# Log-sum-exp of 16,384 rows on one core: another list of loads (twenty in place of nineteen), with other groups of rows for each engine

## The chip, the core and the metric

The kernel runs on one core of a Trainium2 chip. The core's engines run side by side, each with its own instruction stream, and meet through semaphores: ScalarE (ACT in the profile) does exponentials and logarithms, VectorE (DVE) sums, GpSimd (POOL) adds, TensorE (PE) has only three tiny products at the end, and SyncE (SP) issues the transfers from memory. The metric is the time of one execution on the device in microseconds; lower is better.

## The reference

```python
x = np.random.randn(32, 512, 1024).astype(np.float32)

max_x = np.max(x, axis=-1, keepdims=True)
out = max_x.squeeze(-1) + np.log(np.sum(np.exp(x - max_x), axis=-1))
```

There are 32 x 512 = 16,384 rows of 1024 floats, 67.1 MB, and one float comes out per row. The kernel sums exp(x) without the maximum, checks at the end that all sums lie within sane bounds, and has a second, slower way with the maximum that runs only where the check fails. With this input it isn't run.

## The kernel before, in words

The 16,384 rows are spread over the 128 partitions of the on-chip memory, 128 rows to a partition. Below, "a row" is one row in every partition: 1024 elements wide, 512 KB in all. Rows 0 to 111 of each partition come from one block of the input (`x_rows`), rows 112 to 127 from a second (`x_rest`).

The plan is a list, `LOADS`, of pairs: how many rows a transfer brings (fractions are allowed, in steps of 1/32), and in a string what is done with rows once they are there. A load may end within a row; the next one brings the rest. The loop over the list (`for i, (size, parts) in enumerate(loads)`) writes out the instruction streams of all engines:

- **SyncE** issues one transfer per load (line 143), in the list's order, into `ring`, a buffer of 48 rows (`RING`). Loads are laid one behind the other; where the next does not fit any more, it goes to the ring's start. Before it issues a load, SyncE waits until every earlier row in that space has been summed (the list `users`). All loads go through one queue and their data move in the order of issue.
- **ScalarE** waits for a load to land and puts exp over it in place (line 231), in one instruction for each part of the string that the load's text has, separated by blanks. A `+` joins several groups in one exponential, with the groups behind it. The last part of a load takes all that has landed, fractions of a row included.
- **Letters.** `R9`: VectorE sums nine whole rows with one reduction (line 242). `G7`: GpSimd adds the second half of seven rows to the first (line 237), and a later `H` makes VectorE sum the halves of all groups folded until then (line 161); only then is their ring space free. `T2`: VectorE adds the halves of a row and sums them in one `scalar_tensor_tensor` per row (line 169). `C`: VectorE checks the sums so far, two small reductions (line 178). `L`: ScalarE takes the logarithm of rows 0 to 111 (line 204), for which it waits until VectorE has summed the last of them; SyncE then stores these results early, after all loads. `a` and `b`: the two pieces of the last row; VectorE sums the first, and ScalarE sums the second as it takes its exponential (line 226).

At load number `HELD` (counted from 0) VectorE waits, before its T instruction, for the next load to land too.

Behind the loop come the logarithms of the last 16 rows (lines 269 and 271), the store, and the check of the sums: lines 280 and 284 on VectorE, three products on TensorE (lines 290 to 294) and the comparison of line 298. Each engine works its instructions in the order in which they are written: a ScalarE instruction that waits holds up all behind it. Nothing plans at run time; the list is the whole schedule.

Of the kernel before, what the change touches and what calls it, by code (L numbers as in the profile page):

```python
# [10 lines left out]
RING = 48  # L11
B = 16

HELD = 15

# [2 lines left out]


LOADS = [
# [5 lines left out]
]  # L28


# [23 lines left out]
def kernel(  # L54
# [127 lines left out]
    for i, (size, parts) in enumerate(loads):  # L182
# [8 lines left out]
        for k, part in enumerate(parts):  # L191
# [41 lines left out]
            for how, s in part:  # L233
# [12 lines left out]
                elif how == "T":  # L246
                    if i == HELD:
                        nc.vector.wait_ge(landed[i + 1], 16)
# [161 lines left out]
```

## Time and profile before

| | us |
|---|---|
| median of 3 runs | 161.41 (161.4 to 161.55) |
| the profiled execution | 161.56 |
| its span | 160.2 |
| VectorE busy | 116.1 |
| ScalarE busy | 114.5 |
| GpSimd busy | 33.3 |
| transfers into and out of the core, 67.18 MB | mean 419 GB/s over the span |

The span runs from the first recorded instruction to the last; about 1.3 us of the execution lie around it. Rows of the timeline give the start and the duration in us, engine, line, operation, output and input with their sizes, how many instructions the row holds, and in brackets the engine's idle time before it with what ended it. A row that stands for several instructions names the first one's size. GpSimd and ScalarE rows name the elements per partition: 1024 for a whole row, 512 for a half. The stage rows give, for each stretch, busy time and instruction count of PE, PEld (TensorE's loading of weights), DVE, ACT and POOL, the clock granted to TensorE, the busy share of the DMA engines and the GB/s.

### The profile page before, as it was taken

What the parts mean: (1) busy time and instruction counts of PE and PEld (TensorE: products, weight loads), DVE (VectorE), ACT (ScalarE), POOL (GpSimd) and SP (SyncE); (2) the same over time, 40 slices, a digit from 0 to 9 for tenths busy, and PEclk for the clock granted to TensorE, in tenths of its full rate; (3) what the DMA queues carried; (4) which work ended last, traced back from release to release, by engine and by line L of the source; (5) the groups of instructions that cost most, each with busy time, mean ns of one, the idle gap of its engine ahead of it and who ended that gap; (6) DMA issues with size and microseconds to landing.
All of it is one profiled execution on the core that took longest, in us unless ns stands there. A gap on an engine that the chain in (4) does not pass through costs nothing.

```text
span 160.2 us, 183 instructions
## 1 busy us (share of the span) xinstructions
PE 0.3 (0%) x6; PEld 0.2 (0%) x6; DVE 116.1 (72%) x56; ACT 114.5 (71%) x32; POOL 33.3 (21%) x14
## 2 busy tenths in 40 slices
PE   0000000000000000000000000000000000000000
PEld 0000000000000000000000000000000000000000
DVE  0000000029998499999999799929989999999996
ACT  3000069970899519992799449964998999999996
POOL 0000000000000000000000000990580489996000
DMA  8999799799699699997999999997999999999992
GB/s 288 479 511 431 336 514 450 321 514 497 272 512 512 288 463 478 478 448 312 424 467 467 467 429 429 429 429 332 498 426 409 415 440 394 438 419 425 417 408 101
DMA packets 3025, 67.18 MB, mean 419 GB/s; under 512 B 592, under 2 KB 720, under 8 KB 1488
## 3 DMA queue, kind: packets, MB, share of 16 engines
q1 hardware_dynamic: 3024, 67.18, 97.9%
q14 instruction: 1, 0.01, 0.0%
HBM read 67.11 MB, written 0.07 MB: 419 GB/s over the span
## 4 chain that ended last, share of the span: by engine, by line
DMA 54%; DVE 21%; ACT 19%; POOL 5%; issue 0%; PE 0%; SPq 0%
DMA ring<-in_x_dram 54%; ACT ring L231 19%; DVE sumexp L242 15%; POOL ring L237 5%; DVE ring L169 3%; DVE sumexp L161 2%; SPq L143 0%; DVE clamped L280 0%; PE count L290 0%; ACT res L204 0%; DVE fine L298 0%; PE count L292 0%; PE count L294 0%
## 5 line engine op out<-in xcount | busy, mean ns | idle before, releaser
L231 ACT ACTIVATE ring<-ring 128x16000 f32<-128x16000 f32 (+24 forms) x25 | 112.2, 4546 | 42.8 <-DMA ring<-in_x_dram 42.8
L242 DVE TENSOR_REDUCE sumexp<-ring 128x9 f32<-128x9216 f32 (+7 forms) x10 | 89.8, 9000 | 39.2 <-ACT ring L231 39.2
L237 POOL TENSOR_TENSOR ring<-ring 128x2048 f32<-128x2048 f32 (+5 forms) x8 | 33.0, 4135 | 112.3 <-ACT ring L231 112.3
L161 DVE TENSOR_REDUCE sumexp<-ring 128x4 f32<-128x2048 f32 (+5 forms) x8 | 16.5, 2080 | 3.5 <-POOL ring L237 3.5
L169 DVE SCALAR_TENSOR_TENSOR ring<-ring 128x512 f32<-128x512 f32 (+1 forms) x16 | 9.8, 671 | 0.0
L130 ACT ACT_TABLE_LOAD x1 | 1.3, 1283 | 1.4 <-PEq L63 1.4
L169 DVE DVE_READ_ACCUMULATOR ring<-ring 128x1 f32 x16 | 1.3, 82 | 0.0
L226 ACT ACTIVATE unused<-ring 128x480 f32<-128x480 f32 x1 | 0.6, 559 | 0.0
L290 PE MATMUL count<-far,bad 128*1 128x1 f32 x2 | 0.2, 164 | 158.7 <-DVE clamped L280 158.7
L178 DVE TENSOR_REDUCE sumexp<-sumexp 128x1 f32<-128x106 f32 x2 | 0.4, 258 | 0.0
L298 DVE TENSOR_SCALAR fine<-count 1x1 int32<-1x1 f32 x1 | 0.1, 146 | 0.3 <-PE count L294 0.3
L131 POOL MEMSET ones<- 128x1 f32 x1 | 0.1, 98 | 1.0 <-POOLq L63 1.0
L290 PEld LDWEIGHTS count<-far,bad 128*1 128x1 f32 x2 | 0.1, 80 | 158.7 <-DVE clamped L280 158.7
L204 ACT ACTIVATE res<-sumexp 128x112 f32<-128x112 f32 x1 | 0.3, 279 | 0.0
L271 ACT ACTIVATE res<-rest,sumexp 128x1 f32<-128x1 f32 x1 | 0.3, 261 | 0.0
L280 DVE SCALAR_TENSOR_TENSOR clamped<-sumexp 128x23 f32<-128x23 f32 x1 | 0.2, 183 | 0.0
L269 ACT ACTIVATE res<-sumexp 128x15 f32<-128x15 f32 x1 | 0.2, 205 | 0.0
L292 PE MATMUL count<-total,ones 128*1 128x1 f32 x2 | 0.2, 164 | 0.0
L294 PE MATMUL count<-sumexp,ones 128*1 128x1 f32 x2 | 0.2, 164 | 0.0
L284 DVE TENSOR_REDUCE total<-sumexp 128x1 f32<-128x24 f32 x1 | 0.2, 173 | 0.0
L274 ACT COPY sumexp<-rest 128x1 f32<-128x1 f32 x1 | 0.2, 152 | 0.0
L394 POOL MEMSET const-float32-0.0<- 128x1 f32 x1 | 0.1, 98 | 0.2 <-issue 0.2
(8 smaller groups left out, 0.8 us busy)
## 6 DMA issues: line engine op xcount, KB each, us to landing
ring<-in_x_dram SPq DMA_DIRECT2D x1, 8048.0 KB, 39.1
ring<-in_x_dram SPq DMA_DIRECT2D x1, 8016.0 KB, 57.6
ring<-in_x_dram SPq DMA_DIRECT2D x1, 8000.0 KB, 21.5
ring<-in_x_dram SPq DMA_DIRECT2D x1, 7472.0 KB, 25.8
ring<-in_x_dram SPq DMA_DIRECT2D x1, 7312.0 KB, 22.9
ring<-in_x_dram SPq DMA_DIRECT2D x1, 6720.0 KB, 21.5
ring<-in_x_dram SPq DMA_DIRECT2D x1, 5200.0 KB, 17.6
ring<-in_x_dram SPq DMA_DIRECT2D x1, 3584.0 KB, 19.1
```

What stands on the lines that cost most here:

```text
L130: nc.scalar.preload_act_table_set("natural_log_exp_and_others")
L161: at = dve.did(nc.vector.reduce_sum(out=sumexp[:, c0 : c0 + s], in_=half, axis=AX.X))
L169: return nc.vector.scalar_tensor_tensor(out=lo, in0=lo, scalar=1.0, in1=v[:, h : 2 * h], op0=ALU.mult, op1=ALU.add, accum_out=sumexp[:, co ...
L178: dve.did(nc.vector.tensor_reduce(out=sumexp[:, col : col + 1], in_=sumexp[:, 0:c], op=op, axis=AX.X))
L204: ln_early = act.did(nc.scalar.activation(out=res[:, 0:W], in_=sumexp[:, 0:W], func=AF.Ln))
L226: nc.scalar.activation(out=unused[:, 0 : upto - here], in_=v, func=AF.Exp, accum_out=rest).then_inc(parts_summed, 1)
L231: at = act.did(nc.scalar.activation(out=v, in_=v, func=AF.Exp))
L237: folded.append((c, p, s, pool.did(nc.gpsimd.tensor_tensor(out=rows[:, :, 0:H], in0=rows[:, :, 0:H], in1=rows[:, :, H:d], op=ALU.add,))))
L242: users.append((p, p + s * d, dve, dve.did(nc.vector.reduce_sum(out=sumexp[:, c : c + s], in_=rows, axis=AX.X))))
L269: act.did(nc.scalar.activation(out=res[:, W:LAST], in_=sumexp[:, W:LAST], func=AF.Ln))
L271: ln_last = act.did(nc.scalar.activation(out=res[:, LAST:NC], in_=rest, func=AF.Ln, bias=sumexp[:, LAST:NC]))
L290: pe.did(nc.tensor.matmul(count, lhsT=bad, rhs=far, start=True, stop=False))
```

## The change

The list is another. The ring, the letters and the code behind the list are the same.

```diff
-HELD = 15
+HELD = 16
...
 LOADS = [
-    (15.625, "R15"), (15.71875, "R16"), (15.65625, "R9 R7"), (14.59375, "R14"),
-    (14.28125, "G7 H R7"), (13.125, "G5 H R9"), (10.15625, "G4 H R3+G3 H"), (7, "G4 R2 H G1"),
-    (5.84375, "H C G2+R1 G3 H"), (4.46875, "T4"), (3.09375, "T3 L"), (2.40625, "T2"),
-    (1.75, "T2"), (1.25, "T1"), (0.75, "T1"), (0.65625, "T1"), (0.625, "T1"), (0.53125, "a"),
-    (0.46875, "b"),
+    (15.71875, "R15"), (15.3125, "R16"), (15.96875, "R16"), (14.5625, "G5 R9 H"),
+    (15.625, "R7+G2 R7 H"), (10.8125, "R11"), (7.5, "G5 G2"), (8.0625, "H G5 R3"),
+    (4.03125, "G3 G1 H C"), (4.40625, "G1 T4 H"), (4.3125, "R2+G2 L H"), (3.03125, "T3"),
+    (2.40625, "T2"), (1.6875, "T2"), (1.3125, "T1"), (0.96875, "T1"), (0.75, "T1"),
+    (0.59375, "T1"), (0.5, "a"), (0.4375, "b"),
 ]
```

There are 20 loads; the first three fill 47 rows of the ring as before, the next three now 41 (before 42), and the list goes to the ring's start twice, as before. Of the 127 rows that are not split, VectorE sums 86 with whole-row reductions (before 83), GpSimd folds 26 (before 29), its first at load 3 (before load 4), and 15 are T rows in both; four of these now come in load 9, ahead of the groups of load 10. Load 2 is one group of 16 rows, with one exponential, in place of nine and seven. The early logarithm `L` stays in load 10, which now holds two whole and two folded rows in place of three T rows. The check at the end takes one column less, since the early check `C` covers one more row.

## The prediction

> **What bounds the kernel now.** First the page's span and busy times, then the timeline of ScalarE alone, because every load is first touched by an exponential there: a row that ends its idle time on the DMA tells when a load was ready.
>
> ```profile
> span 160.2 us, 183 instructions
> ...
> PE 0.3 (0%) x6; PEld 0.2 (0%) x6; DVE 116.1 (72%) x56; ACT 114.5 (71%) x32; POOL 33.3 (21%) x14
> ```
>
> ```profile
> 21.56 13.54 ACT L231 ACTIVATE ring<-ring 128x16000 f32<-128x16000 f32 x1 [18.83 <-DMA ring<-in_x_dram]
> 40.54 13.62 ACT L231 ACTIVATE ring<-ring 128x16096 f32<-128x16096 f32 x1 [5.45 <-DMA ring<-in_x_dram]
> 59.45 13.66 ACT L231 ACTIVATE ring<-ring 128x8864 f32<-128x8864 f32 x2 [5.29 <-DMA ring<-in_x_dram]
> 77.09 12.66 ACT L231 ACTIVATE ring<-ring 128x14944 f32<-128x14944 f32 x1 [3.98 <-DMA ring<-in_x_dram]
> 94.34 12.48 ACT L231 ACTIVATE ring<-ring 128x6560 f32<-128x6560 f32 x2 [4.60 <-DMA ring<-in_x_dram]
> 110.25 11.50 ACT L231 ACTIVATE ring<-ring 128x4224 f32<-128x4224 f32 x2 [3.42 <-DMA ring<-in_x_dram]
> 122.53 15.22 ACT L231 ACTIVATE ring<-ring 128x4096 f32<-128x4096 f32 x5 [0.79 <-DMA ring<-in_x_dram]
> 138.08 5.28 ACT L231 ACTIVATE ring<-ring 128x2912 f32<-128x2912 f32 x2 [0.33 <-DMA ring<-in_x_dram]
> 143.52 6.75 ACT L231 ACTIVATE ring<-ring 128x4576 f32<-128x4576 f32 x2 [0.16 <-DMA ring<-in_x_dram]
> 150.18 0.28 ACT L204 ACTIVATE res<-sumexp 128x112 f32<-128x112 f32 x1
> 150.37 7.55 ACT L231 ACTIVATE ring<-ring 128x2464 f32<-128x2464 f32 x7
> 157.82 0.56 ACT L226 ACTIVATE unused<-ring 128x480 f32<-128x480 f32 x1
> 158.31 0.13 ACT L226 ACTIVATION_READ_ACCUMULATOR unused<-ring 128x1 f32 x1
> ```
>
> The transfers never pause. Load 1 (15.71875 rows) becomes ready 18.98 us after load 0, load 2 (15.65625) 18.91 us later, load 4 (14.28125) 17.25 us after load 3, load 6 (10.15625) 12.28 us after load 5. One straight line fits: 1.2055 us a row and 0.04 us a load (15.71875 x 1.2055 + 0.04 = 18.99; 10.15625 x 1.2055 + 0.04 = 12.28). From load 9 (143.52) to load 18 lie 11.53 rows in nine loads, by the line 14.26 us, so the last is ready at 157.78 at the earliest; ScalarE starts it at 157.82. The bound is the queue of loads, not an engine: the end is 157.8 plus a tail that nearly cannot shrink. What a change of the list can do is delay the queue (a load issued too late) or lengthen the tail (an engine behind when the last load lands).
>
> The tail is two paths. ScalarE's ends at 158.31 + 0.13 = 158.44. VectorE's, from its own timeline:
>
> ```profile
> 157.40 0.69 DVE L169 SCALAR_TENSOR_TENSOR ring<-ring 128x512 f32<-128x512 f32 x1
> 158.01 0.08 DVE L169 DVE_READ_ACCUMULATOR ring<-ring 128x1 f32 x1
> 158.01 0.44 DVE L169 SCALAR_TENSOR_TENSOR ring<-ring 128x272 f32<-128x272 f32 x1
> ```
>
> It ends at 158.45. Behind both stand 1.75 us of checks and control to 160.2. So the span is (later of the two paths) + 1.75. The profiled execution took 161.56 us for its span of 160.2; the median of the runs is 161.41, 0.15 below it. I work out a difference in span and put it on 161.41.
>
> **The change, part by part: the queue.** The same 128 rows come in 20 loads instead of 19: + 0.04 us by the line. Between no cost and what an issue not hidden would cost (bounded below), 0.04 is what nineteen loads showed. Ready times in the changed kernel are 21.56 + (rows loaded - 15.625) x 1.2055 + 0.04 x load number: load 2 at 59.46, load 3 77.05, load 4 95.93, load 5 109.00, load 6 118.09, load 7 127.85, load 8 132.75, load 9 138.10, load 10 143.34, then 147.04, 149.98, 152.05, 153.67, 154.88, 155.82, 156.58, 157.22 and 157.79 for load 19.
>
> That holds if SyncE issues each load before the queue reaches it, which hangs on ring space freed by VectorE. Its rows, and the page's issue rows for loads 4 and 5:
>
> ```profile
> 35.13 16.15 DVE L242 TENSOR_REDUCE sumexp<-ring 128x15 f32<-128x15360 f32 x1 [35.13 <-ACT ring L231]
> 54.19 34.41 DVE L242 TENSOR_REDUCE sumexp<-ring 128x16 f32<-128x16384 f32 x3 [2.91 <-ACT ring L231]
> 89.78 15.09 DVE L242 TENSOR_REDUCE sumexp<-ring 128x14 f32<-128x14336 f32 x1 [1.18 <-ACT ring L231]
> 107.91 3.89 DVE L161 TENSOR_REDUCE sumexp<-ring 128x7 f32<-128x3584 f32 x1 [3.05 <-POOL ring L237]
> 111.72 7.61 DVE L242 TENSOR_REDUCE sumexp<-ring 128x7 f32<-128x7168 f32 x1
> 119.73 2.82 DVE L161 TENSOR_REDUCE sumexp<-ring 128x5 f32<-128x2560 f32 x1 [0.41 <-POOL ring L237]
> 122.47 9.75 DVE L242 TENSOR_REDUCE sumexp<-ring 128x9 f32<-128x9216 f32 x1
> ...
> 141.43 2.87 DVE L161 TENSOR_REDUCE sumexp<-ring 128x4 f32<-128x2048 f32 x2
> 144.34 0.43 DVE L178 TENSOR_REDUCE sumexp<-sumexp 128x1 f32<-128x106 f32 x2
> 144.69 1.21 DVE L242 TENSOR_REDUCE sumexp<-ring 128x1 f32<-128x1024 f32 x1
> ```
>
> ```profile
> ring<-in_x_dram SPq DMA_DIRECT2D x1, 7312.0 KB, 22.9
> ring<-in_x_dram SPq DMA_DIRECT2D x1, 6720.0 KB, 21.5
> ```
>
> Before, load 4 (7312 KB) was under way for 22.9 us though it takes 17.25: 5.6 us of it in the queue; load 5 likewise 21.5 - 15.9 = 5.6. That is the spare now. After: load 2 is one R16 in place of R9 and R7, so ScalarE works it in one piece. By its rows (13.62 for 16096 elements, 12.66 for 14944: 0.833 ns an element and 0.2 us) that ends at 59.46 + 13.82 = 73.28, and VectorE, idle from about 70.7, reduces 16 rows in 17.22 (1.07 us a row + 0.12, from 9.75 for 9 and 7.61 for 7) to 90.5. Load 5 waits for exactly this and the queue needs it at 95.93: 5.4 us spare. Load 4 needs the first R16, about 70.7 (load 1 is 0.4 us earlier ready), against 77.05. Load 6 needs R9 and the folded five of load 3: 90.5 + 9.67 + 2.8 = 102.9 against 109.00. Loads 11 to 19 need R11, about 131.4, against 143.34 and later. So no load starves. VectorE's 2.6 us of idle time in front of R16 are covered by these spares; without them each microsecond beyond would shift the end by one. SyncE's own row before:
>
> ```profile
> 132.24 10.66 SPq L143 DMA_DIRECT2D ring<-in_x_dram  x7
> ```
>
> Seven issues in 10.66 us, 1.5 each; nine from 131.4 at that pace end at 145.1, twelve microseconds before the last is needed. The early store is queued behind them; it is issued after L204, 147.3 in place of 150.5, and in both kernels its data stand in the queue behind the last load.
>
> **VectorE up to the early logarithm.** L204 now stands in load 10 and waits for the last folded row of load 9, and behind it on ScalarE are the eight exponentials of loads 11 to 18 and the last, which everything waits for. So VectorE's chain counts. Steps from the rows above, an instruction starting 0.08 before its forerunner ends (107.91 + 3.89 = 111.80 against 111.72): R of n rows 1.07n + 0.04; H of n folded rows 0.535n + 0.065 (3.89 for 7, 2.82 for 5); the early check 0.47 (the reduction before it ends at 144.30, less the 0.08, to 144.69); a T row 0.61. The chain starts when ScalarE has done the R7+G2 piece of load 4, 8640 elements: 95.93 + 7.40 + 0.03 = 103.36. Then R7 7.53, R7 7.53, H2 1.14, R11 11.81, H5 2.74, H2 1.14, R3 3.25, H5 2.74, H3 1.67, H1 0.60, check 0.47, T4 2.44, H1 0.68 with its end: 43.74, ending at 147.10. GpSimd has to keep up:
>
> ```profile
> 100.09 7.79 POOL L237 TENSOR_TENSOR ring<-ring 128x3584 f32<-128x3584 f32 x1 [98.52 <-ACT ring L231]
> ...
> 131.57 11.57 POOL L237 TENSOR_TENSOR ring<-ring 128x1536 f32<-128x1536 f32 x4 [0.78 <-ACT ring L231]
> 143.44 3.44 POOL L237 TENSOR_TENSOR ring<-ring 128x1536 f32<-128x1536 f32 x1 [0.29 <-ACT ring L231]
> ```
>
> That is 1.09 us a row + 0.18. G5 of load 7 starts when ScalarE's 4608 elements are done, 131.96, and ends at 137.6, G3 141.0, the two G1 142.25 and 143.5; VectorE comes to H3 at 141.24, 0.2 later. R3's exponential ends at 135.02, VectorE comes at 135.25. So the chain holds, with 0.2 us at its two tightest places.
>
> **ScalarE to the end.** A step is 0.833 ns an element + 0.1 us: the row of seven has 8160 elements, 6.80 us, in 7.55. Load 10 starts at 143.34, its 4416 elements step to 147.12; L204 needs VectorE's 147.10 + 0.03 = 147.13: nothing lost. L204 steps 0.19 (150.18 to 150.37), to 147.32. Then 3104 to 150.01, 2464 to 152.16, 1728 to 153.70, 1344 to 154.92, 992 to 155.84, 768 to 156.58, 608 to 157.18 (load 18 is ready at 157.22), 512 to 157.75, and the last load at 157.79: ScalarE is 0.3 us behind at load 11 and caught up by load 18. Its path ends 0.62 - 0.03 (32 elements fewer) later, at 158.38. VectorE: T of load 16 at 156.68, T of load 17 at 157.30 to 157.92, the half row of load 18 in 0.45: 158.37. The wait moved from load 15 to 16 (for load 17 to land, 156.58) is over before ScalarE hands over that row at 156.65; it costs nothing.
>
> **Sum.** 158.38 against 158.45: - 0.07 us. 161.41 - 0.07 is 161.34; I say 161.35, no change that a measurement tells from none (within 0.2%, 0.32 us, is about what it can).
>
> **A rule of the skill.** T4 in load 9 is the change's riskiest move by row: its `scalar_tensor_tensor` runs right behind GpSimd's last G1 (143.98 against 143.5), while before the first T, behind the rows above, came 1.7 us after GpSimd's last end at 146.88. The Trainium skill, page "SBUF — State Buffer", section "Who interferes with whom", says that a VectorE instruction with two SBUF inputs and a GpSimd instruction that reads SBUF lock each other out for a whole instruction, while a reduction does not contend. The trace of before agrees as far as it goes: R9 beside GpSimd took 9.75, as its rate elsewhere; it has no T beside GpSimd. By the rule and by the rows the sum is the same as long as the two keep those 0.5 us apart; where they do not, the rule gives rival 2.
>
> **The rivals.** (1) Slower: VectorE's 43.7 us chain runs late and L204 holds ScalarE. It decides from 0.1 us of lateness on (0.03 at load 18, 0.04 at the last load), then one to one; 1% of the chain, 0.44, gives 161.7, 1 us of it 162.25; I take 161.9. For it: the two 0.2 us spares, no idle time after 103.4. Against: reductions in the trace go by one line. (2) Slower: GpSimd is late by over 0.5 us and T4 and G1 exclude each other; H1 then ends up to one G1 later (1.27): 161.8 to 162.5. Nothing in the trace makes GpSimd late, and no row of before shows the two side by side. (3) Slower: the queue pays for the added load or for late space. The nearest row for a price from above is an issue's 1.5 us: 162.9; against it stands the 0.04 and the 5.4 us spare. (4) Faster: the queue loses time in the middle, which other sizes recover:
>
> ```profile
> 94.34:110.25 15.91, 0.00 (x0) 0.00 (x0) 12.86 (x2) 12.49 (x3) 7.79 (x1) 1.00 0.97 420
> 110.25:122.53 12.28, 0.00 (x0) 0.00 (x0) 11.87 (x4) 11.49 (x2) 5.65 (x1) 1.00 0.97 419
> ```
>
> A DMA share of 0.97 over 28.2 us would be 0.85 us, giving at best 160.5. Against it: these stages keep to the line within 0.05 us.
>
> **How the numbers follow.** The forecast has 0.75, (1) 0.10, (2) 0.05, (3) 0.04, (4) 0.06. The likeliest case's own range is 161.2 to 161.6; the range 161.15 to 161.95 takes in most of rival 1 and leaves out about 2 in 10. Faster by over 0.2% is (4), 0.06; slower (1) to (3), 0.19; the rest 0.75.
>
> **What would show it.** ScalarE's rows: load 4 ready at 95.9, load 10 at 143.3, the last exponential starting at 157.8. L204 at 147.1. VectorE idle about 0.5 us before 103.4 and not again until 147. If L204 starts after 147.3 rival 1 holds; a T longer than 0.7, rival 2; a last load ready after 158, rival 3.

## The result and the profile after

| | before | after |
|---|---|---|
| median of 22 runs each, us | 161.52 | 161.72 |
| profiled execution, us | 161.56 | 161.78 |
| its span, us | 160.2 | 160.4 |

The ratio is 1.0014, 95% interval [1.0008, 1.002]: slower by 0.2 us, where a gain of 0.07 was forecast. It is less than the 0.2% that was called no change, and 161.72 is inside the wide range, but it lies above the 161.2 to 161.6 of the likeliest case, it is a change clear of noise, and it has the other sign. The span of the page and the timeline of ScalarE after the change:

```profile
span 160.4 us, 186 instructions
```

```profile
21.65 13.62 ACT L231 ACTIVATE ring<-ring 128x16096 f32<-128x16096 f32 x1 [18.91 <-DMA ring<-in_x_dram]
40.10 13.27 ACT L231 ACTIVATE ring<-ring 128x15680 f32<-128x15680 f32 x1 [4.84 <-DMA ring<-in_x_dram]
59.40 13.83 ACT L231 ACTIVATE ring<-ring 128x16352 f32<-128x16352 f32 x1 [6.03 <-DMA ring<-in_x_dram]
77.07 12.72 ACT L231 ACTIVATE ring<-ring 128x5120 f32<-128x5120 f32 x2 [3.84 <-DMA ring<-in_x_dram]
95.95 29.54 ACT L231 ACTIVATE ring<-ring 128x8640 f32<-128x8640 f32 x5 [6.16 <-DMA ring<-in_x_dram]
127.92 14.75 ACT L231 ACTIVATE ring<-ring 128x4608 f32<-128x4608 f32 x6 [2.44 <-DMA ring<-in_x_dram]
143.47 3.88 ACT L231 ACTIVATE ring<-ring 128x4416 f32<-128x4416 f32 x1 [0.80 <-DMA ring<-in_x_dram]
147.26 0.28 ACT L204 ACTIVATE res<-sumexp 128x112 f32<-128x112 f32 x1
147.45 10.65 ACT L231 ACTIVATE ring<-ring 128x3104 f32<-128x3104 f32 x8
158.02 0.55 ACT L226 ACTIVATE unused<-ring 128x448 f32<-128x448 f32 x1
158.51 0.13 ACT L226 ACTIVATION_READ_ACCUMULATOR unused<-ring 128x1 f32 x1
```

The idle times ended by the DMA give the ready times. Forecast and measured: load 4 at 95.93 and 95.95, load 7 at 127.85 and 127.92, load 10 at 143.34 and 143.47, the last at 157.79 and 158.02. The shortfall grows load by load, 0.02, 0.07, 0.13, 0.23: the queue itself is slower than the line said. From load 4 to the last lie 50.81 rows in 15 loads; 62.07 us less 50.81 x 1.2055 leave 0.82, which is 0.054 us a load in place of 0.04 (the first three landings came 0.02 to 0.07 earlier than forecast, so the loss begins behind them).

The engines did what was worked out for them. From VectorE's timeline, and the row of GpSimd behind which its first T stands:

```profile
103.39 15.15 DVE L242 TENSOR_REDUCE sumexp<-ring 128x7 f32<-128x7168 f32 x2 [0.52 <-ACT ring L231]
...
143.93 0.68 DVE L169 SCALAR_TENSOR_TENSOR ring<-ring 128x512 f32<-128x512 f32 x1
...
146.38 0.68 DVE L161 TENSOR_REDUCE sumexp<-ring 128x1 f32<-128x512 f32 x1
147.39 2.29 DVE L242 TENSOR_REDUCE sumexp<-ring 128x2 f32<-128x2048 f32 x1 [0.33 <-ACT ring L231]
...
158.15 0.08 DVE L169 DVE_READ_ACCUMULATOR ring<-ring 128x1 f32 x1
158.15 0.45 DVE L169 SCALAR_TENSOR_TENSOR ring<-ring 128x288 f32<-128x288 f32 x1
```

```profile
132.04 11.51 POOL L237 TENSOR_TENSOR ring<-ring 128x2560 f32<-128x2560 f32 x4 [0.77 <-ACT ring L231]
```

Its long chain ran from 103.39 to 147.06 (forecast 103.36 to 147.10), and L204 did not wait for it: ScalarE came to L204 at 147.26 only because load 10 was late. The paths end at 158.51 + 0.13 = 158.64 on ScalarE and 158.60 on VectorE, against 158.45 before; what follows is 1.75 to 1.8 us again. All of the loss stands in front of the last load's exponential.

### The profile page after: what moved, and what is told of

Same layout as the page of the kernel before. It is cut to its first block, busy times and chain, and to the rows that moved or that the text cites. A ratio compares the mean times of both kernels' runs of the same rounds, so it can differ in the third digit from the quotient of the medians.

```text
span 160.4 us, 186 instructions
## 1 busy us (share of the span) xinstructions
PE 0.3 (0%) x6; PEld 0.2 (0%) x6; DVE 117.9 (73%) x56; ACT 114.5 (71%) x32; POOL 30.2 (19%) x15
## 4 chain that ended last, share of the span: by engine, by line
DMA 54%; ACT 22%; DVE 21%; issue 0%; SPq 0%; PE 0%
DMA ring<-in_x_dram 54%; ACT ring L231 22%; DVE sumexp L242 20%; DVE sumexp L161 1%; ACT unused L226 0%; SPq L143 0%; DVE clamped L280 0%; PE count L290 0%; ACT res L204 0%; DVE fine L298 0%; PE count L292 0%; PE count L294 0%; SPq L50 0%
## 5 line engine op out<-in xcount | busy, mean ns | idle before, releaser
L231 ACT ACTIVATE ring<-ring 128x5120 f32<-128x5120 f32 (+23 forms) x25 | 112.3, 4548 | 43.0 <-DMA ring<-in_x_dram 43.0
L242 DVE TENSOR_REDUCE sumexp<-ring 128x16 f32<-128x16384 f32 (+6 forms) x9 | 92.9, 10341 | 40.7 <-ACT ring L231 40.7
L237 POOL TENSOR_TENSOR ring<-ring 128x2560 f32<-128x2560 f32 (+3 forms) x9 | 29.8, 3330 | 118.4 <-ACT ring L231 118.4
L161 DVE TENSOR_REDUCE sumexp<-ring 128x5 f32<-128x2560 f32 (+3 forms) x9 | 14.9, 1685 | 0.2 <-POOL ring L237 0.2
L226 ACT ACTIVATE unused<-ring 128x448 f32<-128x448 f32 x1 | 0.5, 548 | 0.0
L204 ACT ACTIVATE res<-sumexp 128x112 f32<-128x112 f32 x1 | 0.3, 279 | 0.0
```

The lines of the kernel that those rows point to most:

```text
L161: at = dve.did(nc.vector.reduce_sum(out=sumexp[:, c0 : c0 + s], in_=half, axis=AX.X))
L204: ln_early = act.did(nc.scalar.activation(out=res[:, 0:W], in_=sumexp[:, 0:W], func=AF.Ln))
L226: nc.scalar.activation(out=unused[:, 0 : upto - here], in_=v, func=AF.Exp, accum_out=rest).then_inc(parts_summed, 1)
L231: at = act.did(nc.scalar.activation(out=v, in_=v, func=AF.Exp))
L237: folded.append((c, p, s, pool.did(nc.gpsimd.tensor_tensor(out=rows[:, :, 0:H], in0=rows[:, :, 0:H], in1=rows[:, :, H:d], op=ALU.add,))))
L242: users.append((p, p + s * d, dve, dve.did(nc.vector.reduce_sum(out=sumexp[:, c : c + s], in_=rows, axis=AX.X))))
```

## The experiments

For the comparisons below the landings of single loads were read from the trace's records: a load has landed when the last of the 16 DMA engines has reported its part. A fixed 1.20586 us a row is taken off; what a kernel needs beyond that from the first landing to the last is called its surplus. Nearly the same rows lie behind the first load in every list (all but those of the first three loads cut in twelve), so another rate would shift these surpluses alike. Before has 0.73 us for its 18 further loads, the changed kernel 0.98 for 19. The first landing differs by up to half a microsecond between executions (21.25 to 21.72 in those below, for nearly one size), so a single surplus is good to about 0.1. Much of that is one late engine: as a mean over the engines the first landings lie within 0.2 us, and the two profiles of a kernel that was run twice agree to 0.03. The times, each from 6 to 12 runs beside 26 to 34 of before, decide.

**Once more, and with the tail of before.** `after_again` is the changed kernel itself. `body_after_tail_before` takes the loads after row 112 from the list before:

```diff
-    (4.3125, "R2+G2 L H"), (3.03125, "T3"), (2.40625, "T2"), (1.6875, "T2"), (1.3125, "T1"),
-    (0.96875, "T1"), (0.75, "T1"), (0.59375, "T1"), (0.5, "a"), (0.4375, "b"),
+    (4.46875, "T4"), (3.09375, "T3 L"), (2.40625, "T2"), (1.75, "T2"), (1.25, "T1"),
+    (0.75, "T1"), (0.65625, "T1"), (0.625, "T1"), (0.53125, "a"), (0.46875, "b"),
```

> The changed kernel once more, unaltered, for a second profile. Against the prediction, its profile had the last load ready at 158.00 us in place of 157.79, while every engine stood where it was forecast. Theory N (chance: the slowest DMA engine was hit more often in that one execution): the last load is ready anywhere between 157.8 and 158.0, and the median lies 0.0 to 0.1 us above before. Theories P (a load costs the queue more than 0.04 us) and S (some sizes cost more): ready at 158.0 again, the median 0.2 us above before.

> Loads 0 to 9 of the changed list, then loads 9 to 18 of the list before: 20 loads, the tail sizes of before. Theory P (one price per load): as the changed kernel, + 0.2 us on before. Theory S (the changed tail's sizes cost more): within 0.1 us of before, last load ready at 157.8 to 157.85. A third, Theory M (the loads of the middle, numbers 6 to 9 of the changed list, cost more): + 0.1 to 0.2 us, with the surplus in the profile already there at load 10.

Measured: `after_again` 1.0013 [1.0004, 1.0022], 0.16 us above before, surplus 0.985 as in the first profile (0.98). The last load was ready at 157.85, because the first landing came 0.15 us earlier; that moment alone would have fitted Theory N, but the median and the surplus speak against chance. With the other tail 1.0009 [1.0, 1.0018], 0.15 above before, surplus 0.875, of which 0.42 were there at load 9 (the changed kernel: 0.45). In that profile about half of the surplus over before goes with the tail, at the same 20 loads, but the difference of 0.1 is no more than a single surplus is good for and the medians of the two kernels agree. That is a hint against a price by count alone, and decides neither for the tail nor for the middle alone.

**The price of a load, nine times over.** Before, with its first three loads as twelve (`HELD` goes from 15 to 24 with them); in a second version the twelve have other sizes:

```diff
-    (15.625, "R15"), (15.71875, "R16"), (15.65625, "R9 R7"),
+    (4, "R4"), (4, "R4"), (4, "R4"), (3.625, "R3"), (4, "R4"), (4, "R4"), (4, "R4"),
+    (3.71875, "R4"), (4, "R4"), (4, "R4"), (4, "R4"), (3.65625, "R4"),
...
```

```diff
+    (4.03125, "R4"), (4.0625, "R4"), (4.0625, "R4"), (3.5, "R3"), (4.0625, "R4"), (4.0625, "R4"),
+    (4.0625, "R4"), (3.5, "R4"), (4.0625, "R4"), (4.0625, "R4"), (4.0625, "R4"), (3.46875, "R4"),
...
```

> Before, with its first three loads (47 rows) brought as twelve, all but three of 4 rows: 28 loads, everything behind unchanged. The price of a load, nine times over. Theory P at 0.2 us a load: + 1.8 us. At the prediction's 0.04: + 0.36 us. At 0.055, what the changed kernel's landings give: + 0.5 us. Theories S and M: + 0.3 to 0.4 us.

> As first_in_12, but the twelve loads have sizes of 4.0625, 3.5 and so on, so that their pieces start and end at other multiples of 128 bytes. Theory S: more than first_in_12, by 0.2 us or more (12 loads at 10 to 25 ns each, twice the surplus seen). Theories P and M: the same as first_in_12 within 0.1 us.

Measured: 1.0033 [1.0021, 1.0046] and 1.0024 [1.0014, 1.0034], 0.53 and 0.37 us for nine loads more: 0.06 and 0.04 us a load. A price of 0.2 a load (Theory P) is out. Theory S was wrong in its sign: the odd sizes are the cheaper ones, by 0.16 us in the median, which Theories P and M did not have either. The single landings of the first of the two told more. Beyond the rows' time its loads 2 to 6 (4 rows, one of 3.625) cost 69 to 82 ns each, loads 8 to 10, of 4 rows too, only 9 to 20. What differs is where they lie: behind load 7 with its 3.71875 rows, all ends are shifted by an odd number of 1/32 rows, that is of 128 bytes. Sorted this way the landings so far fell into three groups, with much scatter within each, and a new theory was formed, E in the expectations below.

**Ends moved by 128 bytes.** `after_odd` moves ten of the changed list's ends, `before_even` the ten odd ends of the list before, each by 1/32 row; groups and number of loads stay. Beside them before ran again. Of each edit the first changed line is shown:

```diff
-    (15.96875, "R16"), (14.5625, "G5 R9 H"), (15.625, "R7+G2 R7 H"), (10.8125, "R11"), (7.5, "G5 G2"),
+    (15.96875, "R16"), (14.59375, "G5 R9 H"), (15.625, "R7+G2 R7 H"), (10.78125, "R11"), (7.53125, "G5 G2"),
...
```

```diff
-    (15.625, "R15"), (15.71875, "R16"), (15.65625, "R9 R7"), (14.59375, "R14"), (14.28125, "G7 H R7"),
+    (15.625, "R15"), (15.75, "R16"), (15.625, "R9 R7"), (14.625, "R14"), (14.25, "G7 H R7"),
...
```

> Theory E (ends): count where each load ends in steps of 1/32 row, 128 bytes of a partition. In the landings so far a load that begins and ends at an even count cost some 72 ns beyond 1.20586 us a row, one that begins and ends at an odd count some 18, a mixed one some 45; where the cheap ones come in a row the price stays at about 40, that of the reading side. The changed list has 13 even and 6 odd ends inside, the list before 8 and 10. This run is the changed list with ten of its even ends moved by 1/32 row to odd ones (3 even left), the number of loads and the groups as they were. Theory E: from the first landing to the last 0.75 to 0.80 us beyond the rows' time in place of 0.98; the last load 0.2 us earlier after the first, the median within 0.06 us of before. Theory P (price by count alone): 0.98 again, + 0.15 to 0.2 us on before.

> The list before with its ten odd ends moved by 1/32 row to even ones: still 19 loads. Theory E: 18 ends at 72 ns, 1.3 us beyond the rows' time in place of 0.73; median + 0.4 to 0.6 us on before, slower than the changed kernel. Theory P: 19 loads as before, no difference (within 0.06 us).

> Before, unaltered, for a second profile. Theory E: 0.73 us beyond the rows' time from the first landing to the last, as in the first profile, to 0.03 us; the moment of the first landing may vary by 0.1. If it varies more than that, the surplus of the changed kernel is no property of its list.

Measured: `before_even` 1.0024 [1.0013, 1.0034], 0.4 us slower with the same 19 loads, surplus 1.17 (Theory E had 1.3): the count of loads can't be the cause of that. `after_odd` 1.0007 [0.9997, 1.0017], a median 0.05 above before in place of 0.16 to 0.2; its interval overlaps that of the changed kernel, so alone it decides nothing. Its profile does not bear the theory out: one landing there, load 10, came 0.32 us late on the slowest of the DMA engines, and the surplus is 1.16 in place of 0.75 to 0.80; as a mean over the engines it is 0.93 against 1.01 and 1.03 in the two profiles of the changed kernel. `before_again` has 1.0 [0.9991, 1.0009], with the last load ready at 157.76 as in the first profile (157.78). Its surplus is 0.85, not 0.73 to 0.03, and its first landing moved by 0.14, more than the 0.1 that was allowed. By the expectation's own words the surplus of one profile then says little about a list, and it can't carry the argument; as a mean over the engines the two profiles of before have 0.85 and 0.83. What carries it are the times, and the two pairs with the moved ring below. ScalarE's timeline of `before_even`:

```profile
94.21 12.46 ACT L245 ACTIVATE ring<-ring 128x6528 f32<-128x6528 f32 x2 [4.56 <-DMA ring<-in_x_dram]
110.10 11.50 ACT L245 ACTIVATE ring<-ring 128x4224 f32<-128x4224 f32 x2 [3.44 <-DMA ring<-in_x_dram]
122.45 15.24 ACT L245 ACTIVATE ring<-ring 128x4096 f32<-128x4096 f32 x5 [0.85 <-DMA ring<-in_x_dram]
138.04 5.26 ACT L245 ACTIVATE ring<-ring 128x2880 f32<-128x2880 f32 x2 [0.34 <-DMA ring<-in_x_dram]
143.54 6.75 ACT L245 ACTIVATE ring<-ring 128x4608 f32<-128x4608 f32 x2 [0.24 <-DMA ring<-in_x_dram]
150.20 0.28 ACT L218 ACTIVATE res<-sumexp 128x112 f32<-128x112 f32 x1
150.38 7.80 ACT L245 ACTIVATE ring<-ring 128x2496 f32<-128x2496 f32 x7
158.09 0.53 ACT L240 ACTIVATE unused<-ring 128x448 f32<-128x448 f32 x1
```

Load 4 is ready 0.13 us earlier than in the first profile of before (94.34), and the last exponential starts 0.27 later (158.09 against 157.82).

**Which side: the ring moved by 128 bytes.** An end has an address in the input and one in the ring. A tile that nobody uses, ahead of the ring, moves only the second (and the small tiles behind the ring with it):

```diff
+    pad = sbuf("pad", 32)
     ring = sbuf("ring", RING * d)
```

With 64 in place of 32 it moves the ring by 256 bytes, as a control.

> The changed kernel with an unused tile of 128 bytes ahead of the ring, so that all ends change between odd and even in the on-chip memory but not in the input. Theory E with the price on the on-chip side: 13 odd and 6 even, 0.75 to 0.80 us beyond the rows' time, median within 0.06 us of before. With the price on the input's side: no difference to the changed kernel, 0.98. Theory P: 0.98 too.

> The run with the 128-byte tile once more, beside its control with 256 bytes. Theory E, on-chip side: 0.77 us beyond the rows' time again, 0.15 to 0.2 us faster than the control, within 0.06 us of before.

> The changed kernel with an unused tile of 256 bytes ahead of the ring: the layout moves, the ends stay odd or even as in the changed kernel. Theory E, on-chip side: as the changed kernel, 0.98 us beyond the rows' time, + 0.15 to 0.2 us on before. If any tile ahead of the ring helps, whatever its size: 0.77, as with 128 bytes.

> The list of before_even (all 18 inner ends even) with the tile of 128 bytes ahead of the ring, which makes all 18 odd in the on-chip memory. Theory E, on-chip side: from 1.17 us beyond the rows' time to 0.70 to 0.77, what the reading side alone takes for 18 loads; the median goes from 0.4 us above before to within 0.1 us of it, perhaps 0.1 below. If the sizes themselves cost (Theory S): 1.17 and + 0.4 us as without the tile.

> Before with the tile of 128 bytes ahead of the ring: its 10 odd and 8 even ends change sides. Theory E, on-chip side: 10 even and 8 odd, 0.05 to 0.15 us slower than before. If the tile helps as such: faster than before by 0.2 us.

Measured: the changed kernel with 128 bytes 1.0003 [0.9994, 1.0012] and, again, 0.9996 [0.9988, 1.0005], surplus 0.77 and 0.75; with 256 bytes 1.0013 [1.0004, 1.0021], surplus 0.98. `before_even` with 128 bytes went from 1.0024 to 1.0003 [0.9994, 1.0012], surplus 1.17 to 0.69. The end of ScalarE's timeline there, to be held against that of `before_even` above:

```profile
143.47 6.75 ACT L246 ACTIVATE ring<-ring 128x4608 f32<-128x4608 f32 x2 [0.18 <-DMA ring<-in_x_dram]
150.13 0.28 ACT L219 ACTIVATE res<-sumexp 128x112 f32<-128x112 f32 x1
150.31 7.57 ACT L246 ACTIVATE ring<-ring 128x2496 f32<-128x2496 f32 x7
157.79 0.53 ACT L241 ACTIVATE unused<-ring 128x448 f32<-128x448 f32 x1
```

The last load landed at 157.67, 0.1 us earlier than in before, but ScalarE reached it only at 157.79, about when before starts its own (157.82): in that profile the queue's gain is lost to ScalarE. ScalarE's timelines of the changed kernel with 128 and with 256 bytes, the second run with 128:

```profile
95.88 29.54 ACT L247 ACTIVATE ring<-ring 128x8640 f32<-128x8640 f32 x5 [6.14 <-DMA ring<-in_x_dram]
127.81 14.75 ACT L247 ACTIVATE ring<-ring 128x4608 f32<-128x4608 f32 x6 [2.38 <-DMA ring<-in_x_dram]
143.24 3.88 ACT L247 ACTIVATE ring<-ring 128x4416 f32<-128x4416 f32 x1 [0.69 <-DMA ring<-in_x_dram]
...
147.22 10.57 ACT L247 ACTIVATE ring<-ring 128x3104 f32<-128x3104 f32 x8
157.77 0.55 ACT L242 ACTIVATE unused<-ring 128x448 f32<-128x448 f32 x1
```

```profile
96.04 29.54 ACT L247 ACTIVATE ring<-ring 128x8640 f32<-128x8640 f32 x5 [6.18 <-DMA ring<-in_x_dram]
128.04 14.75 ACT L247 ACTIVATE ring<-ring 128x4608 f32<-128x4608 f32 x6 [2.46 <-DMA ring<-in_x_dram]
143.57 3.88 ACT L247 ACTIVATE ring<-ring 128x4416 f32<-128x4416 f32 x1 [0.78 <-DMA ring<-in_x_dram]
...
147.55 10.67 ACT L247 ACTIVATE ring<-ring 128x3104 f32<-128x3104 f32 x8
158.13 0.54 ACT L242 ACTIVATE unused<-ring 128x448 f32<-128x448 f32 x1
```

From load 4 to the last it is 61.89 us with 128 bytes and 62.09 with 256: 0.042 and 0.056 us a load. The list, the sizes, the number of loads and the addresses in the input are the same in both. So the price lies with the address in the ring, and a list that looked 0.2 us worse is worth as much as the old one when the ring starts 128 bytes further on. With `before_ring_128` the expected 0.05 to 0.15 us did not show: 0.9999 [0.9991, 1.0008], an interval that leaves room for 0.05 but not for 0.15. Its surplus is 1.02, and as a mean over the engines 0.94, some 0.1 above before, which is the theory's way; but its first landing on the slowest engine came early (21.25), and the last load was ready at 157.78 as in before. Whether ten dear ends in place of eight cost anything in that list stays open. No version beat the kernel before by more than the interval.

The runs beside each other, with the count of ends that are of the dear kind in the ring (even, and odd where the 128-byte tile is in front):

| run | dear ends of all | surplus, us | mean over the engines | median less that of before, us |
|---|---|---|---|---|
| `before_even_ring_128` | 0 of 18 | 0.69 | 0.71 | + 0.03 |
| `after_odd` | 3 of 19 | 1.16 | 0.93 | + 0.05 |
| `after_ring_128`, again | 6 of 19 | 0.77, 0.75 | 0.76, 0.75 | + 0.03, + 0.01 |
| before, again | 8 of 18 | 0.73, 0.85 | 0.85, 0.83 | 0, + 0.01 |
| `before_ring_128` | 10 of 18 | 1.02 | 0.94 | + 0.03 |
| `body_after_tail_before` | 10 of 19 | 0.88 | 0.89 | + 0.15 |
| after, again | 13 of 19 | 0.98, 0.985 | 1.01, 1.03 | + 0.20, + 0.16 |
| `after_ring_256` | 13 of 19 | 0.98 | 1.01 | + 0.24 |
| `before_even` | 18 of 18 | 1.17 | 1.21 | + 0.42 |

The many dear ends at the foot are slower, but the upper five rows do not differ in time: the count of dear ends is no exact price for a list.

## Why the prediction was right and wrong

- **The bound: right.** The last exponential starts within 0.05 us of its load's landing in all profiles but two; in `before_even` it is 0.09 and in `before_even_ring_128` 0.12, where ScalarE came late. The 0.2 us between before and after are the queue's: the last landing is at 157.78 and 158.00.
- **The queue's price, "+ 0.04 us by the line": wrong, and the failed step.** The line had been fitted to the list before, and its 0.04 us a load was carried over as a property of the queue. It depends on where the loads end in the ring: before 0.041 and 0.047, after 0.052 in both profiles, with all ends on the dear side 0.065, with the ring moved by 128 bytes 0.038 to 0.041 for the changed list and `before_even`, but 0.057 for before (surplus over the number of further loads). Nineteen times 0.01 is the missing 0.2 us. The count of loads, the only thing that the step looked at, was the smaller part: with the ring moved by 128 bytes twenty loads take as long as nineteen. The scatter was there in before: its loads 5 and 16, between two dear ends, had cost 75 and 68 ns, loads 7 and 12 to 14, between two of the others, 10 to 28.
- **No starved load: right.** VectorE's chain, which frees the ring, ran as worked out to within 0.05 us, and no single load of the changed kernel cost more than 0.11 us beyond its rows' time.
- **VectorE's chain, the early logarithm, ScalarE to the end: right.** 43.67 us measured for 43.74; ScalarE came to the early logarithm 0.14 us late (147.26 for 147.12), because load 10 was late, and was caught up at the last load, as forecast.
- **Rivals.** Number 1 (VectorE late) and number 2 (T and GpSimd side by side) did not happen: the first T starts at 143.93, 0.4 us after GpSimd's last, and takes 0.68. The Trainium skill's rule on the shared ports (page "SBUF — State Buffer", section "Who interferes with whom") was not put to the test; no run here shows it. Number 4: the changed list recovered nothing, and the earliest last landing of any version, 157.67, is 0.1 us ahead of before, far from the 0.85 that a share of 0.97 seemed to offer. Number 3 was the right place, the queue's price, but at 0.2 us, not at an issue's 1.5. That 1.5 was misread besides: the row of seven issues holds five of 0.33 to 0.47 us and two of 4.56 and 3.71, so it is the price of neither kind. The nine issues of the changed kernel ran from 131.48 to 142.27.
- **Before itself** measured 161.52 over 22 runs, 0.11 above the median of 3 that the forecast was put on; so of the 0.37 us between 161.35 and 161.72 about 0.11 is that base, and the difference forecast, - 0.07, has to be set against + 0.2.

## What to carry to other kernels

A constant taken from a straight-line fit holds for the sizes and addresses it was fitted on; before it is carried to another list, look at the scatter of the single points, which here had the two prices in it. In a kernel bound by its transfers, check the alignment of every piece in the on-chip buffer, not only the number of pieces: here 128 bytes of padding were worth 0.2 us with the changed list and 0.4 with `before_even`, and nothing with the list before; a further load costs about 0.04. Put differences of a few tenths of a microsecond to the test with a change that moves one thing, such as an unused tile, and with a control that moves it by a harmless amount.

## What the runs showed of the hardware

In the programs built from these kernels the ring starts at byte 16,512 of each partition, 128 past a multiple of 256; the "even" ends, the dear ones, are therefore those that lie off a multiple of 256 bytes on the chip, and the 128-byte tile puts them on one (16,640). A load is 128 pieces, one for each partition, spread over 16 DMA engines. With all inner ends off the multiple a load cost 65 ns beyond its rows' time (`before_even`), with all of them on it 38 (`before_even_ring_128`), the list and the addresses in the input being the same. A fit through all single landings of the fourteen profiles, at 1.205 us a row, gives 68 ns for a load between two ends off the multiple, 55 where one is off and 35 where none is. The 72 and 18 of Theory E, taken from few landings, were too far apart.

The Trainium skill, page "DMA: Bandwidth & Descriptors", section "How a descriptor splits into AXI transactions", says that a piece is cut at multiples of 256 bytes and that one which starts off such a multiple moves bytes that nobody uses. That fits the direction; the section tells it of reads, and here moving the written side alone made the difference.

The records also show where a part of the price is paid. The last byte's transfer and the landing that the semaphore reports lie 0.30 to 0.35 us apart for the first three loads of `before_even` and of the versions with the 128-byte tile; in `before_even` that distance grows load by load to 0.52 and is 0.46 at the last, while with the tile it stays at 0.28 to 0.37 for the changed list and for `before_even`. At the last load that is 0.17 of the 0.48 us of surplus between `before_even` with and without the tile. That the writes fall behind the reads is the reading that suggests itself; it was not tried apart. Nor was the input alone moved by 128 bytes. The landings give a hint: loads with both ends on the multiple in the ring cost 27 ns on average where their ends are odd in the input (51 loads, versions without the 128-byte tile) and 37 where they are even (40 loads, with it), so no price of the input's side shows there. Why loads of the cheap kind cost about 40 ns when they come in a row, which the expectations put down to the reading side, is open.
